# Query/key casts ahead of their differences, later steps for a pair's second head, and small VectorE/GpSimd jobs exchanged in a fused attention, conv and MLP trunk

## The chip, the cores and the metric

The kernel runs on one core of a Trainium2 chip. The metric is device time in microseconds (us) of one launch, lower is better. The engines are TensorE (PE in the profile, its weight loads PEld), VectorE (DVE), ScalarE (ACT), GpSimd (POOL) and SyncE (SP), which here issues nearly all transfers. SBUF and PSUM are the on-chip memories; only PE writes matmul results, into PSUM.

## The reference

A trunk of two residual layers on 512 rows of 1024 float32 features. Layer 0 mixes with attention, layer 1 with a short gated convolution, and each is followed by a squared-ReLU MLP. The part that the change touches is layer 0's attention: three groups with their own q, k and v for 16 heads of 64.

```python
D_MODEL = 1024; SEQ = 512; HEAD_DIM = 64
A_HEADS = 16; A_WINDOWS = (128, 512, 2048); A_DILATIONS = (1, 4, 16); A_GROUPS = 3

def mixer_a(h, w_qkv, q_gain, k_gain, w_o, cos, sin):
    qkv = (h @ w_qkv).reshape(B, S, A_GROUPS, 3, A_HEADS, HEAD_DIM)
    for g in range(A_GROUPS):
        dil = A_DILATIONS[g]
        radius = A_WINDOWS[g] // (2 * dil)
        q = partial_rope(rms_norm(qkv[:, :, g, 0], q_gain[g]), cos, sin)
        k = partial_rope(rms_norm(qkv[:, :, g, 1], k_gain[g]), cos, sin)
        v = qkv[:, :, g, 2]
        num, den, mx = dilated_group(q, k, v, dil, radius)   # banded attention
    mx = jnp.stack(mxs, 0)
    wts = jnp.exp(mx - jnp.max(mx, axis=0, keepdims=True))
    num = jnp.sum(wts[..., None] * jnp.stack(nums, 0), axis=0)
    den = jnp.sum(wts * jnp.stack(dens, 0), axis=0)
    return (num / den[..., None]).reshape(B, S, D_MODEL) @ w_o
```

partial_rope turns the first 16 dimensions of a head. The three groups share one softmax: each has its row maximum, and their numerators and denominators are weighted and added.

## The kernel before

Every large product is made in three matmuls: a float32 operand is kept as two fp32r tiles, a rounded high part and a low part (the difference), and high x high, high x low and low x high are added up in PSUM. Weights come from HBM through SP (`wraw`), ACT casts them to the high part `wh` (L292), GpSimd subtracts to make the low part `wl` (L293, called with the engine as an argument), and PE uses both. There are four `wraw` buffers and six of `wh` and `wl`.

The attention runs over 8 pairs of heads. A pair has three units of 8 k-tiles x 4 row groups r x 3 matmuls of 384 columns (L128): unit A makes q0, k0 and q1 (the digit is the group), unit B makes k1, q2 and k2, unit V makes the three v. Between these matmuls stand the small steps of the same and of the previous pair:
- `evacA`, `evacB`, `evacV` copy a unit's results from PSUM (`g`, 4 buffers) to SBUF: `rawA`, `rawB`, and the two halves of `v`. evacV calls `split`: a cast on ACT (L295), then a difference on DVE (L296).
- `norm_sq`, `norm_rs` and `norm_mul` do the RMS norm and the rotary turn, 4 row groups r each (L363 to L382). A number in the table says how many of the 4 have their turn on GpSimd (pA, pB).
- `qk_fill` transposes one of the six on PE (L391) and splits it into high and low part (ACT L295, DVE L296). k1 and k2 go into the diagonal quarters of a tile whose other quarters are zero (`zeros`), so they are split in two halves of 64 partitions each, and k0 in two pieces of 448 and 64 columns.
- `S0`, `S12` are scores (L444, L458), `exps` their exponentials (L467), `spread` and `swap` (L425, L434) bring group 0's statistics into the other groups' row order with small matmuls against a constant, `weigh1` to `weigh3` make the common softmax weights, and `weights_back` swaps group 0's part back.
- `pnorm` scales the 16 blocks of probabilities of a pair by those weights: on GpSimd (L503) or DVE (L505), 12 and 4 in the kernel before.
- `PT` transposes a scaled block (L517) and splits it into `pth` and `ptl`, `PV` multiplies it with v into `o` (L545; one buffer), for head 0 in four steps, then for head 1 in four. After a head's last PV, ACT copies half of `o` out (`tmpO`, L548), and DVE adds the two halves into `oT` (L549). The next head's first PV needs `o` free.

Everything is written out in one order before the run. Each step has a position (a number on an axis along which A, B and V each take 6, so that 1 is 16 of a unit's 96 matmuls), and a heap emits the steps between the matmuls by position. An engine takes its instructions in that order, so a step emitted early blocks what is behind it on its engine until its inputs are there:

```python
    def at(pos, fn):
        count[0] += 1
        heapq.heappush(tasks, (pos, count[0], fn))
```

The positions are sums of tA or tB (the end of a pair's unit A or B) and offsets in the table `PLACES`: row 0 for the first pair, row 1 for the second to the seventh (the middle pairs), row 2 for the last. TB places the k1, q2 and k2 fills, N0 and N12 the scalings, P, dP, gP and lP the PT and PV steps (start, spacing, extra for the second head, distance from PT to PV), X and lX the first swap, W, lW and lF the weights and the swap back, and tb the six rotary tables (`tables`, L254 and L255 on DVE).

Of the kernel before, what the change touches and what calls it, by code (L numbers as in the profile page):

```python
# [14 lines left out]
AF = mybir.ActivationFunctionType  # L15
ALU = mybir.AluOpType
# [19 lines left out]
def _constants():  # L36
# [10 lines left out]
    for n, b in enumerate((0, 1, 3)):  # L47
# [10 lines left out]


PLACES = [  # L60
    dict(sqA=0.52, rsA=0.95, mulA=2.62, dmA=0.05, TA=6.3, dT=0.2, sqB=0.08, rsB=1.22, mulB=1.8, dmB=0.1, TB=5.0, S0=1.05,
         dS=0.5, E0=2.1, X=4.2, lX=0.6, S12=7.2, dS12=0.3, E12=7.9, dE12=0.2, W=9.5, lW=0.35, lF=0.9, N0=10.85, N12=9.95,
         dN=0.04, P=11.4, dP=0.62, gP=0.4, lP=1.7, qA=0, qB=0, pA=3, pB=3, pN=1, vA=0, vB=8, xq=3.57, dxq=0.29, xs=6.25,
         lg=2.48, dlg=0.43, tb=4.26, dtb=0.21, gc=8.63),
    dict(sqA=0.02, rsA=0.87, mulA=1.79, dmA=0.28, TA=4.8, dT=0.19, sqB=0.17, rsB=0.8, mulB=1.07, dmB=0.12, TB=3.9,
         S0=0.45, dS=0.55, E0=1.1, X=3.1, lX=0.5, S12=6.5, dS12=0.24, E12=7.1, dE12=0.2, W=8.9, lW=0.35, lF=0.9, N0=10.25,
         N12=9.4, dN=0.04, P=10.9, dP=0.66, gP=0.4, lP=1.7, qA=0, qB=0, pA=0, pB=3, pN=1, vA=0, vB=12),
    dict(sqA=0.02, rsA=0.8, mulA=1.1, dmA=0.5, TA=4.5, dT=0.1, sqB=0.19, rsB=0.89, mulB=1.15, dmB=0.2, TB=3.9, S0=0.45,
         dS=0.55, E0=1.1, X=3.1, lX=0.5, S12=6.0, dS12=0.24, E12=6.5, dE12=0.18, W=8.0, lW=0.3, lF=0.7, N0=9.1, N12=8.4,
         dN=0.03, P=9.5, dP=0.36, gP=0.2, lP=0.7, qA=0, qB=0, pA=3, pB=2, pN=1, vA=0, vB=9),  # L70
]


# [1 line left out]
def trunk_kernel(ctx, tc, x, norm1, norm2, wqkv, qgain, kgain, wo, win, conv, wout, w1, w2, c_rope, c_m0, c_m12, out):  # L75
    nc = tc.nc
    pe, act, dve, pool, sync = nc.tensor, nc.scalar, nc.vector, nc.gpsimd, nc.sync
    ctx.enter_context(tc.manual_schedule())

    def ptile(p, shape, dt, name, **kw):  # L80
        return p.tile(shape, dt, name=name, **kw)

    def f32(ap):
        return ap.bitcast(F32)
# [57 lines left out]
    ones = ptile(const, [128, 128], R32, "ones")  # L142
# [38 lines left out]
    xs = dram.tile([KT, 128, S], F32, name="xs")  # L181
# [85 lines left out]

    def zeros(nm, i):
        v = f32(qk[nm][i]).rearrange("p (r h c) -> p r h c", r=4, h=2)
        dve.memset(v[0:64, :, 1], 0.0)  # L270
        dve.memset(v[64:128, :, 0], 0.0)

    box = {}

# [14 lines left out]
    def split(hi, lo, src, scale=None, eng=None):  # L289

        if scale is None:
            act.copy(hi, src)  # L292
            (eng or dve).tensor_sub(lo, src, f32(hi))  # L293
        else:
            act.activation(hi, src, AF.Copy, scale=scale)  # L295
            dve.scalar_tensor_tensor(lo, src, scale, f32(hi), op0=ALU.mult, op1=ALU.subtract)  # L296
# [87 lines left out]
    def qk_fill(raw, w, nm, ty):  # L384
        ps = ptile(psT, [128, 512], F32, "st")
        for r in range(4):
            o = ps[:, 128 * r:128 * r + 128]
            if nm[1] == "0":
                n = 32 if nm[0] == "q" else 16
                o = ps.rearrange("p (b r c) -> p r b c", r=4, c=n)[:, r]  # L390
            pe.transpose(o, raw[r][:, w, :], ident)  # L391
        hi, lo = qk[nm]
        g = cols[:, QG + ty // 2 + 3 * (ty % 2):QG + ty // 2 + 3 * (ty % 2) + 1]
        if nm[0] == "q":
            split(hi, lo, ps, g)
        elif nm == "k0":
            for d0, s0, n in ((0, 64, 448), (448, 0, 64)):
                split(hi[:, d0:d0 + n], lo[:, d0:d0 + n], ps[:, s0:s0 + n], g)
        else:
            for h in range(2):  # L400
                pp = slice(64 * h, 64 * h + 64)
                pv = ps[pp].rearrange("p (r c) -> p r c", r=4)
                hv, lv = (t[pp].rearrange("p (r h c) -> p r h c", r=4, h=2)[:, :, h] for t in (hi, lo))
                split(hv, lv, pv, g[pp])

    def q0v(t, h, b):
        return t[64 * h:64 * h + 64, 128 * b:128 * b + 128]
# [6 lines left out]
    def mx(i, n=1):  # L414

        return mxs[:, i // 8, i % 8:i % 8 + n].rearrange("p a b -> p (a b)")

    N0, D0, N0S, N12, D0S, D12, F0S, F12, NM, EX, F0 = 0, 1, 2, 3, 4, 5, 6, 7, 8, 9, 12  # L420

# [14 lines left out]

    def S0(bp):
        ps = [ptile(psT, [128, 512], F32, "st") for _ in range(2)]
        (qh, ql), (kh, kl) = qk["q0"], qk["k0"]
        for b2 in range(2):  # L440
            b = 2 * bp + b2
            for q, (a, k) in enumerate(((qh, kh), (qh, kl), (ql, kh))):
                for h in range(2):
                    pe.matmul(ps[h][:, 256 * b2:256 * b2 + 256], q0v(a, h, b), k0v(k, h, b), start=(q == 0), stop=(q == 2))  # L444
        for h in range(2):
            for b2 in range(2):
                b = 2 * bp + b2
                dve.tensor_tensor_reduce(out=sm0[:, h, b], in0=ps[h][:, 256 * b2:256 * b2 + 256],
                                         in1=msk0[:, (0, 1, 1, 2)[b]], scale=1.0, scalar=3.0e38, op0=ALU.add, op1=ALU.min,
                                         accum_out=mx(N0)[:, 4 * h + b:4 * h + b + 1])  # L450

    def S12(r):
# [6 lines left out]
        for h in range(2):  # L459
            c = slice(4 * h + r, 4 * h + r + 1)  # L460
            dve.tensor_tensor_reduce(out=sm12[:, h, r], in0=ps[:, 256 * h:256 * h + 256], in1=msk12, scale=1.0,  # L461
                                     scalar=3.0e38, op0=ALU.add, op1=ALU.min, accum_out=mx(N12)[:, c])

    def exps(g, h, b):
        t, m, d = ((sm0, N0, D0), (sm12, N12, D12))[g]
        c = slice(4 * h + b, 4 * h + b + 1)
        act.activation(t[:, h, b], t[:, h, b], AF.Exp, bias=mx(m)[:, c], scale=-1.0, accum_out=mx(d)[:, c])  # L467

    def pair_of(i):
        return mx(i, 2).rearrange("p (g n) -> p g n", g=2)  # L470
# [117 lines left out]
    def attn_tasks(p, tA, tB, c):  # L588
# [25 lines left out]
        for i, nm in enumerate(("k1", "q2", "k2")):  # L614
            put(tB + c["TB"] + c["dT"] * i, "TB", lambda i=i, nm=nm: qk_fill(rawB, i, nm, 3 + i), ("mulB", p, 4),
                ("S12", p - 1, 4))
        for i in range(2):
            put(tS + c["S0"] + c["dS"] * i, "S0", lambda i=i: S0(i), ("TA", p, 3), ("PT", p - 1, 8), ("gains", 0, 11))
            for n in range(4):
                put(tS + c["E0"] + c["dS"] * i + 0.15 * n, "E0", lambda i=i, n=n: exps(0, n // 2, 2 * i + n % 2), ("S0", p, i + 1))  # L620

# [25 lines left out]
    c = PLACES[0]  # L647
# [8 lines left out]
    for kt in range(KT):  # L656
        at(9.0 + 0.4 * kt, lambda kt=kt: sync.dma_start(xs[kt], oT[kt]))
    for i in range(4):
        at(9.0 + 0.7 * i, lambda i=i: zeros(("k1", "k2")[i // 2], i % 2))
    at(7.0, lambda: dve.memset(f32(ones), 1.0))  # L660
    at(8.8, perm_consts)
    for i in range(8):
        at(c["xq"] + c["dxq"] * i, lambda i=i: x_squares(i % 4, i // 4))
    at(c["xs"], x_stats)
# [334 lines left out]
```

## Time and profile before

| what | value |
|---|---|
| median of three runs | 1533.86 us (1533.09 to 1535.66) |
| time of the profiled execution | 1538.26 us |
| its span in the trace | 1536.4 us |
| TensorE busy | 1488.8 us, 97% of the span |
| VectorE, ScalarE, GpSimd busy | 693.0, 664.4, 727.6 us |
| data moved | 144.76 MB, 94 GB/s over the span |

The span goes from the first instruction of the profiled execution to its last. The page gives for each engine its busy time, for PE the granted clock by slices (1.00 is full), and for each wait the tile that ended it and the engine that made that tile. The stages in the trace: up to about 60 us the first unit and its preparations, then the attention pairs up to about 620 us, then the output projection, MLP, convolution and MLP.

### The profile page before, as it was taken

Reading aid. Unit: us, or ns where it says so; the run is one execution under the profiler, and the core shown is the slowest. Engines: PE = TensorE matmul, PEld = TensorE weight load, DVE = VectorE, ACT = ScalarE, POOL = GpSimd, SP = SyncE. Lnnn points to the kernel's source line nnn. Section 1 sums busy time; section 2 is a strip of 40 time slices with the busy share of each in tenths; the row PEclk is TensorE's granted clock in tenths of the full one; section 3 lists DMA queues with packets and bytes.
Section 4 is the critical chain, followed back from the end, with each engine's and each line's share of the span. In section 5 each row is a group of like instructions: output and inputs, shape, how many; then the busy total and the mean of one; then the engine's idle time right before and its main releaser. Section 6 shows DMA issues by size and latency. Waiting matters only on the chain.

```text
span 1536.4 us, 22581 instructions
## 1 busy us (share of the span) xinstructions
PE 1488.8 (97%) x7900; PEld 1296.0 (84%) x7900; DVE 693.0 (45%) x1522; ACT 664.4 (43%) x1364; POOL 727.6 (47%) x760
## 2 busy tenths in 40 slices
PE   8889999999999998999999999999999999999998
PEld 8788989999999997788888888888887888888887
DVE  5747666666657566452112032473347420121222
ACT  6445554645555555444443242433333443433320
POOL 3543544445463654354444444455454544444542
PEclk9999999999999999999999999999999999999999
DMA  6431323222232322433333333233332333333332
GB/s 149 128 95 53 110 62 100 77 86 83 80 90 63 110 62 94 129 101 99 97 93 100 97 96 96 83 90 100 100 110 82 96 97 96 96 97 96 97 96 82
DMA packets 163293, 144.76 MB, mean 94 GB/s; under 512 B 13748, under 2 KB 123116, under 8 KB 163180
## 3 DMA queue, kind: packets, MB, share of 16 engines
q1 hardware_dynamic: 162892, 143.06, 31.1%
q8 instruction: 62, 1.02, 0.3%
q14 instruction: 51, 0.42, 0.1%
q10 hardware_dynamic: 288, 0.27, 0.1%
HBM read 134.89 MB, written 8.39 MB: 93 GB/s over the span
## 4 chain that ended last, share of the span: by engine, by line
PE 59%; DVE 2%; issue 0%; DMA 0%; ACT 0%; POOL 0%; DVEq 0%
PE g L128 58%; DVE sqa L701 1%; DVE hgBl L703 0%; PE o L545 0%; PE st L517 0%; DVE hT L922 0%; PE g L855 0%; DMA out<-zr 0%; DVE zr L921 0%; PE g L715 0%; POOL sm L503 0%; DVE zr L814 0%; ACT sgh L292 0%; PE g L714 0%; DVE hgl L293 0%
## 5 line engine op out<-in xcount | busy, mean ns | idle before, releaser
L293 POOL TENSOR_TENSOR wl<-wraw,wh 128x512 fp32r<-128x512 f32 (+1 forms) x542 | 637.5, 1196 | 721.4 <-ACT wh L292 714.6
L292 ACT CAST wh<-wraw 128x512 fp32r<-128x512 f32 (+1 forms) x542 | 300.0, 570 | 542.3 <-PE g L128 412.4
L128 PE MATMUL g<-hgBl,wh 128*128 128x512 f32 x704 | 274.9, 390 | 0.0
L128 PE MATMUL g<-hgBh,wl 128*128 128x512 f32 x704 | 274.8, 390 | 0.0
L128 PE MATMUL g<-hgBh,wh 128*128 128x512 f32 x704 | 274.6, 390 | 0.0
L128 PE MATMUL g<-wh,hgh 128*128 128x384 f32 x768 | 265.2, 345 | 6.4 <-DVE v L296 6.4
L128 PE MATMUL g<-wl,hgh 128*128 128x384 f32 x768 | 264.0, 344 | 3.6 <-POOL wl L293 3.6
L128 PE MATMUL g<-wh,hgl 128*128 128x384 f32 x768 | 265.7, 346 | 1.9 <-DVE hgl L307 1.9
L791 DVE SCALAR_TENSOR_TENSOR zr<-g,R 128x512 f32<-128x512 f32 x64 | 44.2, 691 | 293.6 <-PE g L128 293.5
L128 PEld LDWEIGHTS g<-hgBh,wl 128*128 128x128 f32 x704 | 132.7, 188 | 27.9
L128 PEld LDWEIGHTS g<-hgBl,wh 128*128 128x128 f32 x704 | 132.7, 189 | 27.6
L128 PEld LDWEIGHTS g<-hgBh,wh 128*128 128x128 f32 x704 | 132.7, 188 | 27.6
L128 PEld LDWEIGHTS g<-wh,hgh 128*128 128x128 f32 x768 | 145.7, 190 | 9.0 <-DVE v L296 8.7
L128 PEld LDWEIGHTS g<-wl,hgh 128*128 128x128 f32 x768 | 145.9, 190 | 4.8 <-POOL wl L293 4.3
L128 PEld LDWEIGHTS g<-wh,hgl 128*128 128x128 f32 x768 | 145.5, 189 | 5.2 <-DVE hgl L307 3.1
L808 DVE TENSOR_TENSOR acc<-g,acc 128x512 f32<-128x512 f32 x32 | 22.1, 692 | 138.2 <-PE g L128 138.2
L128 PE MATMUL g<-z0h,wh 128*128 128x512 f32 x192 | 74.7, 389 | 0.0
L128 PE MATMUL g<-z0l,wh 128*128 128x512 f32 x192 | 74.7, 389 | 0.0
L128 PE MATMUL g<-z0h,wl 128*128 128x512 f32 x192 | 74.7, 389 | 0.0
L467 ACT ACTIVATE sm<-sm,mxs 128x256 f32<-128x256 f32 x128 | 63.7, 499 | 15.0 <-DVE mxs L461 10.2
L293 DVE TENSOR_TENSOR ptl<-st,pth 128x512 fp32r<-128x512 f32 x64 | 43.9, 688 | 50.9 <-ACT pth L292 50.1
L292 ACT CAST pth<-st 128x512 fp32r<-128x512 f32 x64 | 37.6, 588 | 64.9 <-PE st L517 64.6
(222 smaller groups left out, 2379.3 us busy)
## 6 DMA issues: line engine op xcount, KB each, us to landing
wraw<-in_mlp_w SPq DMA_DIRECT2D x256, 256.0 KB
wraw<-in_a_wqkv SPq DMA_DIRECT2D x128, 128.0 KB
wraw<-in_a_wqkv SPq DMA_DIRECT2D x64, 192.0 KB
wraw<-in_a_wqkv SPq DMA_DIRECT2D x128, 64.0 KB
wraw<-in_b_win SPq DMA_DIRECT2D x64, 128.0 KB
v0d<-v SPq DMA_DIRECT2D x8, 512.0 KB
v<-v0d SPq DMA_DIRECT2D x64, 64.0 KB
wraw<-in_a_wo SPq DMA_DIRECT2D x16, 256.0 KB
```

Source lines behind the costliest of these rows:

```text
L128: pe.matmul(unit["ps"][n][:, :width], a, b, start=st, stop=sp)
L292: act.copy(hi, src)
L293: (eng or dve).tensor_sub(lo, src, f32(hi))
L467: act.activation(t[:, h, b], t[:, h, b], AF.Exp, bias=mx(m)[:, c], scale=-1.0, accum_out=mx(d)[:, c])
L701: dve.tensor_add(state["sqa"], state["sq0"] if n == 1 else state["sqa"], sq)
L791: dve.scalar_tensor_tensor(zr, ps, 0.0, state["R"], op0=ALU.max, op1=ALU.mult)
L808: dve.tensor_add(a, ps, a)
```

## The change

- `qk_fill` first issues the casts of all its pieces on ACT and then all the differences on DVE. Before, a piece's difference stood between its cast and the next piece's cast, in the program's order.
- pN goes from 1 to 2 in all three rows: 8 of a pair's 16 scalings are on GpSimd and 8 on DVE.
- Row 1 (middle pairs): TB 3.9 to 4.05, and the steps of the second head come later (gP 0.4 to 0.9, with dP 0.66 to 0.64 and lP 1.7 to 1.6).
- Row 0 (first pair): unit A's rotary is all on DVE (pA 3 to 0), the tables start at 5.8 and not at 4.26, the k1/k2 fill is at 6.2 and not at 5.0, and S0, E0, S12, E12, W, N12, N0 and P come 0.2 to 0.6 later.
- Row 2 (last pair): unit B's rotary has three of four on GpSimd, the two swaps stand further from their spreads (lX 0.5 to 1.0, lF 0.7 to 1.0), N0 and P are 0.3 later, dP, gP and lP a little shorter.
- The zero fills of k1 and k2 (8 of 64x512 elements) and of `ones` move from DVE to GpSimd, and from positions 9.0 to 11.1 (`ones` 7.0) to 1.0 to 3.25 (`ones` 2.0). `perm_consts` moves from 8.8 to 2.0.

The code parts, and of the table one row:

```diff
@@ PLACES, row 1 @@
-    dict(sqA=0.02, rsA=0.87, mulA=1.79, dmA=0.28, TA=4.8, dT=0.19, sqB=0.17, rsB=0.8, mulB=1.07, dmB=0.12, TB=3.9,
+    dict(sqA=0.02, rsA=0.87, mulA=1.79, dmA=0.28, TA=4.8, dT=0.19, sqB=0.17, rsB=0.8, mulB=1.07, dmB=0.12, TB=4.05, S0=0.45,
...
-         N12=9.4, dN=0.04, P=10.9, dP=0.66, gP=0.4, lP=1.7, qA=0, qB=0, pA=0, pB=3, pN=1, vA=0, vB=12),
+         dN=0.04, P=10.9, dP=0.64, gP=0.9, lP=1.6, qA=0, qB=0, pA=0, pB=3, pN=2, vA=0, vB=12),
...
@@ zeros @@
-        dve.memset(v[0:64, :, 1], 0.0)
-        dve.memset(v[64:128, :, 0], 0.0)
+        pool.memset(v[0:64, :, 1], 0.0)
+        pool.memset(v[64:128, :, 0], 0.0)
@@ qk_fill @@
         if nm[0] == "q":
-            split(hi, lo, ps, g)
+            parts = [(hi, lo, ps, g)]
         elif nm == "k0":
-            for d0, s0, n in ((0, 64, 448), (448, 0, 64)):
-                split(hi[:, d0:d0 + n], lo[:, d0:d0 + n], ps[:, s0:s0 + n], g)
+            parts = [(hi[:, d0:d0 + n], lo[:, d0:d0 + n], ps[:, s0:s0 + n], g) for d0, s0, n in ((0, 64, 448), (448, 0, 64))]
         else:
+            parts = []
             for h in range(2):
                 pp = slice(64 * h, 64 * h + 64)
                 pv = ps[pp].rearrange("p (r c) -> p r c", r=4)
-                hv, lv = (t[pp].rearrange("p (r h c) -> p r h c", r=4, h=2)[:, :, h] for t in (hi, lo))
-                split(hv, lv, pv, g[pp])
+                parts.append(tuple(t[pp].rearrange("p (r h c) -> p r h c", r=4, h=2)[:, :, h] for t in (hi, lo)) + (pv, g[pp]))
+        for h_, l_, v, sc in parts:
+            act.activation(h_, v, AF.Copy, scale=sc)
+        for h_, l_, v, sc in parts:
+            dve.scalar_tensor_tensor(l_, v, sc, f32(h_), op0=ALU.mult, op1=ALU.subtract)
@@ the steps of the first pair @@
-        at(9.0 + 0.7 * i, lambda i=i: zeros(("k1", "k2")[i // 2], i % 2))
-    at(7.0, lambda: dve.memset(f32(ones), 1.0))
-    at(8.8, perm_consts)
+        at(1.0 + 0.75 * i, lambda i=i: zeros(("k1", "k2")[i // 2], i % 2))
+    at(2.0, lambda: pool.memset(f32(ones), 1.0))
+    at(2.0, perm_consts)
```

**Where instructions move.** First ACT's queue in the second pair, at the fills of k1, q2 and k2, with each instruction's waits; before:

```order
L295 ACTIVATE k1h<-st,cols 64x4x128 [waits PE_49]
L295 ACTIVATE k1h<-st,cols 64x4x128 [waits DVE_49]
L295 ACTIVATE q2h<-st,cols 128x512 [waits PE_49]
L295 ACTIVATE k2h<-st,cols 64x4x128 [waits PE_49]
L295 ACTIVATE k2h<-st,cols 64x4x128 [waits DVE_49]
L292 CAST wh<-wraw 128x384 [waits DMAHW4_49,DMAHW3_49,Pool_49]
```

and of the change, the same place:

```order
L405 ACTIVATE k1h<-st,cols 64x4x128 [waits PE_49]
L405 ACTIVATE k1h<-st,cols 64x4x128
L405 ACTIVATE q2h<-st,cols 128x512 [waits PE_49]
L405 ACTIVATE k2h<-st,cols 64x4x128 [waits PE_49]
L405 ACTIVATE k2h<-st,cols 64x4x128
L292 CAST wh<-wraw 128x384 [waits DMAHW4_49,DMAHW3_49,Pool_49]
```

The order is the same, and the second half of k1 and of k2 no longer waits for DVE.

Second, GpSimd's queue at the start of the program, after the identity matrix; `wl` are the weights' low parts and the tiles with a P are the rotary's temporaries of the first pair's unit A. Before:

```order
L293 TENSOR_TENSOR wl<-wraw,wh 128x384 x14
L379 TENSOR_TENSOR tmpR1P<-rawA_108,tabA 128x96
L380 TENSOR_TENSOR tmpR2P<-rawA_108,tabA 128x6x8
L381 TENSOR_TENSOR tmpR2P<-rawA_108,tabA 128x6x8
L382 TENSOR_TENSOR rawA_108<-tmpR1P,tmpR2P 128x6x16
```

and of the change:

```order
L293 TENSOR_TENSOR wl<-wraw,wh 128x384
L270 MEMSET k1h 64x4x128
L271 MEMSET k1h 64x4x128
L293 TENSOR_TENSOR wl<-wraw,wh 128x384
L270 MEMSET k1l 64x4x128
L271 MEMSET k1l 64x4x128
L663 MEMSET ones 128x128
L293 TENSOR_TENSOR wl<-wraw,wh 128x384
L270 MEMSET k2h 64x4x128
L271 MEMSET k2h 64x4x128
...
L293 TENSOR_TENSOR wl<-wraw,wh 128x384 x17
```

Twelve rotary instructions that stood between two runs of `wl` (three row groups of four) are gone from this queue, and nine fills stand between the first `wl`.

Third, DVE's queue in the second pair around the add that frees `o` after the first head; `rawA_109` to `rawA_111` are row groups 1 to 3 of the next pair's unit A, L373 their norm, L379 to L382 their rotary. Before:

```order
L373 TENSOR_TENSOR rawA_110<-rawA_110,stA 128x384
L379 TENSOR_TENSOR tmpR_2423<-rawA_110,tabA 128x96
L380 TENSOR_TENSOR tmpR_2424<-rawA_110,tabA 128x6x8
L381 TENSOR_TENSOR tmpR_2424<-rawA_110,tabA 128x6x8
L382 TENSOR_TENSOR rawA_110<-tmpR_2423,tmpR_2424 128x6x16
L549 TENSOR_TENSOR oT_75<-o,tmpO 64x512
L293 TENSOR_TENSOR ptl<-st,pth 128x512
```

and of the change:

```order
L373 TENSOR_TENSOR rawA_110<-rawA_110,stA 128x384
L379 TENSOR_TENSOR tmpR_2414<-rawA_110,tabA 128x96
L380 TENSOR_TENSOR tmpR_2415<-rawA_110,tabA 128x6x8
L381 TENSOR_TENSOR tmpR_2415<-rawA_110,tabA 128x6x8
L382 TENSOR_TENSOR rawA_110<-tmpR_2414,tmpR_2415 128x6x16
L293 TENSOR_TENSOR ptl<-st,pth 128x512
L552 TENSOR_TENSOR oT_75<-o,tmpO 64x512
L373 TENSOR_TENSOR rawA_111<-rawA_111,stA 128x384
```

The add still stands behind row group 2's rotary, and one `ptl` difference has moved ahead of it. On PE, five matmuls of a unit more stand ahead of the second head's first PV than before.

## Rows read from the trace of the kernel before

**Rows 1.** Windows: length, busy (instructions) of PE, PEld, DVE, ACT, POOL, clock, DMA share, GB/s.

```profile
48.00:60.00 12.00, 6.72 (x32) 5.57 (x30) 8.96 (x21) 3.42 (x8) 8.53 (x14) 0.86 0.50 163
60.00:130.00 70.00, 63.78 (x414) 60.87 (x415) 42.16 (x125) 34.85 (x87) 32.03 (x46) 0.95 0.31 92
130.00:554.00 424.00, 409.93 (x2842) 390.12 (x2841) 276.18 (x776) 234.70 (x566) 209.66 (x300) 1.00 0.29 83
554.00:627.00 73.00, 63.99 (x405) 55.22 (x404) 43.91 (x110) 38.50 (x88) 29.82 (x37) 0.95 0.32 101
627.00:1168.00 541.00, 540.78 (x2382) 446.59 (x2381) 195.79 (x269) 201.75 (x351) 266.29 (x214) 1.00 0.32 97
```

**Rows 2.** Waits of PE: for which tile of which engine; us in total, times, longest.

```profile
PE g L128 <- DVE v L296: 7.6, 8, 1.6
PE o L545 <- DVE oT L549: 6.9, 6, 1.6
PE st L517 <- POOL sm L503: 5.4, 8, 2.9
PE st L434 <- DVE spread L425: 4.4, 3, 2.1
PE g L128 <- POOL wl L293: 3.6, 2, 3.5
...
PE st L391 <- POOL rawB L382: 2.3, 6, 0.4
...
PE g L128 <- DVE hgl L307: 1.9, 2, 1.7
PE st L444 <- ACT k0h L295: 1.6, 1, 1.6
```

**Rows 3.** Timeline, fourth pair: start, duration, instruction [idle before, what ended it].

```profile
292.44 0.69 ACT L295 ACTIVATE k1h<-st,cols 64x512 fp32r<-64x512 f32 x1 [0.81 <-DVE k1l L296]
298.33 0.44 PE L128 MATMUL g<-wh,hgh 128*128 128x384 f32 x1 [0.81 <-DVE v L296]
```

**Rows 4.** Timeline, the scalings and PE's waits for them: first and fourth pair.

```profile
101.61 0.93 PE L517 MATMUL st<-ident,sm 128*128 128x128 f32 x3 [2.94 <-POOL sm L503]
...
312.51 5.14 POOL L503 TENSOR_SCALAR sm<-sm,mxs 128x256 f32<-128x256 f32 x11 [0.57 <-DVE mxs L492]
312.55 1.06 DVE L505 TENSOR_SCALAR sm<-sm,mxs 128x256 f32<-128x256 f32 x2
315.88 0.78 PE L517 MATMUL st<-ident,sm 128*128 128x128 f32 x3 [0.22 <-POOL sm L503]
```

**Rows 5.** Timeline, fourth pair, around the second head's first PV: PE, DVE, GpSimd.

```profile
329.96 0.26 DVE L379 TENSOR_TENSOR tmpR<-rawA,tabA 128x96 f32<-128x96 f32 x1
332.89 2.08 POOL L293 TENSOR_TENSOR wl<-wraw,wh 128x384 fp32r<-128x384 f32 x2 [5.12 <-ACT wh L292]
333.14 0.95 DVE L379 TENSOR_TENSOR tmpR<-rawA,tabA 128x96 f32<-128x96 f32 x1
334.52 0.34 PE L128 MATMUL g<-wh,hgh 128*128 128x384 f32 x1
334.70 0.34 PE L128 MATMUL g<-wl,hgh 128*128 128x384 f32 x1
336.10 0.39 PE L545 MATMUL o<-pth,v 128*128 128x256 f32 x1 [1.06 <-DVE oT L549]
```

**Rows 6.** Timeline, first pair: tables, last low part, first norm, q0's transposes.

```profile
26.32 1.01 DVE L254 TENSOR_TENSOR tabA<-rope,gb 128x32 f32<-128x32 f32 x1
26.61 0.59 ACT L306 COPY oT<-st 128x512 f32<-128x512 f32 x1
28.39 0.73 DVE L307 SCALAR_TENSOR_TENSOR hgl<-oT,cols,hgh 128x512 fp32r<-128x512 f32 x1
45.42 0.56 DVE L373 TENSOR_TENSOR rawA<-rawA,stA 128x384 f32<-128x384 f32 x1
53.19 1.05 PE L391 MATMUL st<-ident,rawA 128*128 128x128 f32 x4
```

More of the change, by code (lines that the diff above doesn't have):

```diff
@@ L60 @@
 PLACES = [
[L61 to L64, printed above, removed]
-    dict(sqA=0.02, rsA=0.87, mulA=1.79, dmA=0.28, TA=4.8, dT=0.19, sqB=0.17, rsB=0.8, mulB=1.07, dmB=0.12, TB=3.9,
-         S0=0.45, dS=0.55, E0=1.1, X=3.1, lX=0.5, S12=6.5, dS12=0.24, E12=7.1, dE12=0.2, W=8.9, lW=0.35, lF=0.9, N0=10.25,
-         N12=9.4, dN=0.04, P=10.9, dP=0.66, gP=0.4, lP=1.7, qA=0, qB=0, pA=0, pB=3, pN=1, vA=0, vB=12),
-    dict(sqA=0.02, rsA=0.8, mulA=1.1, dmA=0.5, TA=4.5, dT=0.1, sqB=0.19, rsB=0.89, mulB=1.15, dmB=0.2, TB=3.9, S0=0.45,
-         dS=0.55, E0=1.1, X=3.1, lX=0.5, S12=6.0, dS12=0.24, E12=6.5, dE12=0.18, W=8.0, lW=0.3, lF=0.7, N0=9.1, N12=8.4,
-         dN=0.03, P=9.5, dP=0.36, gP=0.2, lP=0.7, qA=0, qB=0, pA=3, pB=2, pN=1, vA=0, vB=9),
+    dict(sqA=0.52, rsA=0.95, mulA=2.62, dmA=0.05, TA=6.3, dT=0.2, sqB=0.08, rsB=1.22, mulB=2.1, dmB=0.1, TB=6.2, S0=1.25,
+         dS=0.65, E0=2.4, X=4.2, lX=0.6, S12=7.8, dS12=0.3, E12=8.4, dE12=0.2, W=10.0, lW=0.35, lF=0.9, N0=11.35, N12=10.45,
+         dN=0.04, P=11.9, dP=0.6, gP=0.5, lP=1.6, qA=0, qB=0, pA=0, pB=3, pN=2, vA=0, vB=8, xq=3.57, dxq=0.29, xs=6.25,
+         lg=2.48, dlg=0.43, tb=5.8, dtb=0.3, gc=8.63),
+    dict(sqA=0.02, rsA=0.87, mulA=1.79, dmA=0.28, TA=4.8, dT=0.19, sqB=0.17, rsB=0.8, mulB=1.07, dmB=0.12, TB=4.05, S0=0.45,
+         dS=0.55, E0=1.1, X=3.1, lX=0.5, S12=6.5, dS12=0.24, E12=7.1, dE12=0.2, W=8.9, lW=0.35, lF=0.9, N0=10.25, N12=9.4,
+         dN=0.04, P=10.9, dP=0.64, gP=0.9, lP=1.6, qA=0, qB=0, pA=0, pB=3, pN=2, vA=0, vB=12),
+    dict(sqA=0.02, rsA=0.8, mulA=1.1, dmA=0.5, TA=4.5, dT=0.1, sqB=0.17, rsB=0.8, mulB=1.07, dmB=0.12, TB=4.05, S0=0.45,
+         dS=0.55, E0=1.1, X=3.1, lX=1.0, S12=6.0, dS12=0.24, E12=6.5, dE12=0.18, W=8.0, lW=0.3, lF=1.0, N0=9.4, N12=8.4,
+         dN=0.03, P=9.8, dP=0.34, gP=0.15, lP=0.6, qA=0, qB=0, pA=3, pB=3, pN=2, vA=0, vB=9),
 ]
```

## The prediction, made before the changed kernel was run

> **What bounds the kernel now.** I read the windows by stage first. From 627 us on PE is busy 540.78 of 541 us [rows 1], and the change moves nothing there, so only the attention can gain: length less PE's busy time leaves, of the earlier windows, 424.00 - 409.93 = 14.1 us of PE idle in the six middle pairs, 70.00 - 63.78 = 6.2 around the first pair's scores, 12.00 - 6.72 = 5.3 just before, and 73.00 - 63.99 = 9.0 in the last pair and its tail [rows 1]. The clock column adds to that. A mean of 0.95 over 70 us means about 7 us at 1.2 instead of 2.4 GHz, which costs some 3.5 us; 0.86 over 12 us means 3.4 us at that level, a cost of 1.7; the middle pairs run at 1.00 [rows 1]. Next the list of PE's waits says what each gap waits for [rows 2], and then the timeline of one middle pair what the releaser itself had waited for [rows 3 to 5]. The kernel is bound by PE, with some four short stops in each pair and a cluster of long ones in the first and the last; a term counts only where it takes one of these stops away or makes one.
>
> A stop costs a little more than its idle time: the first matmul behind it takes 0.44 where others take 0.34 [rows 3, 5]. I add 0.1.
>
> **Middle pairs.** *V.* PE stops 0.81 for the low part of v [rows 3], and over all pairs 7.6 in 8 stops, the longest 1.6 [rows 2]. The first pair has that longest one, six middle pairs make 4.9, and 1.1 is left for the last. Before it, ACT stood 0.81 between the halves of k1, for DVE's difference [rows 3], and the same wait stands between the halves of k2; the v casts are behind both in ACT's queue. Without them the casts of v can start up to 1.6 earlier, and DVE's differences, which no longer alternate with ACT, at least 0.8. That covers the 0.81. Gain 0.9 for each of six pairs; if DVE gains less than I think, the bound is nothing.
>
> *Scalings.* GpSimd takes 5.14 / 11 = 0.47 for one, DVE 1.06 / 2 = 0.53 beside it [rows 4]. PE waits 0.22 [rows 4]. GpSimd's eight now end at 312.51 + 3.7 = 316.2, and the block that the first transposes need from it, its fifth, at 314.9. DVE's order is four of group 1 and 2, the copy behind the swap (some 0.2), and two of group 0: 312.55 + 2.1 + 0.2 + 1.0 = 315.8, where PE was ready at 315.88 - 0.22 = 315.7. So DVE becomes the one that is waited for, by about 0.1. Gain 0.2 to 0.3; bounds 0 and 0.5.
>
> *Second head.* PE stops 1.06 for the add that frees `o` [rows 5]; five of these in the middle pairs make 5.3 of the 6.9, and the first pair has the 1.6 [rows 2]. The second head's first PV comes five matmuls later, each started 0.18 after the one before [rows 5]: 0.9. But the add stands behind row group 2's rotary in DVE's queue, and one low part of the probabilities has moved from a place ahead of row group 1 to one right ahead of the add. That part needs a PE transpose which is itself later. DVE there is slow because of GpSimd: the same rotary instruction takes 0.26 alone and 0.95 while two `wl` of 1.04 run [rows 5]. From nothing (the add slides along) to 1.2 (the stop goes) I take 0.5, nearer to nothing than to all, since the add has not moved ahead of anything.
>
> *Against it.* The pair's last PV is now about 0.9 closer to the next pair's first scores. ACT's copy of `o` and DVE's add behind it stand in the two queues ahead of unit B's squares and sums, so the rotary of B ends later, and PE already waits up to 0.4 for it in six pairs [rows 2]. The k1 fill is two matmuls (0.35) later, which takes up part. Cost 0.25, from 0 to 0.9.
>
> Net 0.9 + 0.3 + 0.5 - 0.25 = 1.45 in five pairs and 0.95 in the sixth (it has no second-head stop): **8.2 us**, bounds 3 and 15.
>
> **First pair.** *Up to q0's transposes (at 53.19 before [rows 6]).* The last low part of x started at 28.39, though its input was there at 26.61 + 0.59 = 27.20 [rows 6]; with the tables behind it, PE's stop of 1.7 [rows 2] is 1.1 shorter. The stop of 3.5 for `wl` [rows 2] goes as well, since twelve rotary instructions leave GpSimd's queue. By PE alone q0's transposes would start near 53.2 - 1.1 - 3.6 - 0.3 = 48. They can't: DVE now does everything. The tables start about 2 us later, and they and the rotary run into more `wl`. A table multiplication beside a `wl` takes 1.01 [rows 6], with neighbours of about 0.2; four more such meetings are 3.3 us. The first norm, at 45.42 before [rows 6], then starts near 50.8. Four row groups follow, each a norm of 0.56 [rows 6] and a rotary whose widest instruction is 0.26 [rows 5], together some 1.3, and 0.5 for the end: 56.5. So q0's transposes come 3.3 later than before, and the gains ahead of them are lost in that. If there are no more meetings than before it is nothing; if each rotary meets one as well it is 6.
>
> *Behind them.* The stop of 1.6 for k0's second piece [rows 2] goes with the cast order: 1.8 back, since two stops' refills go. The clock is low after such a stop already; a longer one may cost 0 to 1.7 more, I take 0.4. Together +3.3 - 1.8 + 0.4 = **1.9 us lost**.
>
> *Fills.* Nine fills go to GpSimd ahead of `wl`. They delay `wl` where PE has them six deep, and the low parts of x on DVE might be held by them as table multiplications are by a `wl`, at 0.8 each [rows 6]; I take nothing, since two `wl` are already used up before. The Trainium skill, "SBUF — State Buffer", section "Who interferes with whom", says that a DVE instruction with two SBUF inputs contends with a GpSimd instruction that reads SBUF and not with one that only writes; no row here has a fill on GpSimd beside DVE, and by the rule the term is nothing too.
>
> *Later stops.* V 1.6 + 0.1 [rows 2] goes, as the k1 fill now comes behind v: 1.7. The scalings' stop of 2.94 [rows 4] is that of six GpSimd scalings behind two `wl`; half of it is DVE's now and no `wl` stands between: 3.1 with its neighbours. With it goes the low clock of this window, 3.5 us by the rows above; if a stop of some length stays, so does that. The second head's 1.6 becomes about 0.5: 1.1. Net for the pair 1.7 + 3.1 + 3.5 + 1.1 - 1.9 = **7.5 us**, bounds 1 and 12.
>
> **Last pair.** V: 1.2. The two swaps' stops are 2.1 each (4.4 in three [rows 2]). The first swap now comes behind k1's transposes, 0.5 of a position later (8 matmuls of 0.18, 1.4 us), but those wait for B's rotary themselves: 0.7. The swap back, 0.3 later, gains 0.9. The scalings' stop, 5.4 - 2.94 - 6 x 0.22 = 1.1 [rows 2, 4], goes down to 0.1: 1.0. Its tail behind the last PV has no cover and doesn't change. **3.8 us**, bounds 1 and 6.
>
> **Sum.** 8.2 + 7.5 + 3.8 = 19.5. The profiled execution took 1538.26 (span 1536.4), so it would take 1518.8; the median of the three runs lies 4.4 below it at 1533.86, which gives 1514. What a measurement can tell from no change is 0.2%, 3.1 us.
>
> **The rivals.**
> - *More comes* (chance 0.22). The second-head stop goes fully (0.7 more in five pairs, 3.5), and q0's transposes are no later than before (3.3): 1507. For it: 0.9 of delay against an idle time of 1.06. Against it: the add has the same work ahead of it.
> - *Less comes* (0.15). No gain at the second head (2.5), q0's transposes 3 later still with 1.3 more at 1.2 GHz, a stop of 0.25 at the scalings that stays (2): 1523. For it: every stop that is taken from PE in a pair lets it arrive earlier at the next one.
> - *The scalings shut each other out* (0.07). If a DVE scaling can't run while GpSimd's run, DVE's four more in a pair end about 1 us later than I have, and PE waits for them: 8 us, 1522. Against it: DVE did two in 1.06 while GpSimd kept to 0.47 each [rows 4]. The Trainium skill, same page and section, has the rule: copies and tensor_scalar can run on DVE in a mode with the port pair it shares with GpSimd, and the one that issues second blocks fully until the other's instruction ends. The trace shows at most some sharing, as said.
> - *Slower* (0.06). One mechanism: the end of the second head, moved towards the next pair's scores, pushes unit B's squares, rotary and k1 fill back in every pair. I priced this at 0.25. To cancel the rest it must cost (19.5 + 7 x 0.25) / 7, about 3 us a pair; at 4 us the time is 1514 + 7 x 3.75 = 1540. Only the queue order of ACT speaks for it; the stop at that place is 0.4 [rows 2], and PE stops there for nothing else.
>
> My forecast has 0.50. The range from 1504 to 1525 holds it and the first three rivals, and leaves out the slower one and the far ends of the bounds. Faster: all but the slower case and a rest of 0.04 that falls within 0.2%.
>
> **What would show it.** In the trace of the changed kernel: no stop of PE for v; k1's and k2's casts back to back; the stop at the second head's first PV near 0.6; stops for `rawB` of about 0.6; a stop of several us for `rawA` before q0's transposes and a low clock behind it; no long stop for scalings in the first pair and a clock near 1.00 in its window; the last pair's swaps near 1.2. The prediction is wrong if the first pair's scalings still stop PE long enough to bring the clock down, if a stop appears at a scaling on DVE in every pair, or if `rawB` costs PE over 1 us a pair.

## The result and the profile after

The changed kernel takes 1515.35 us (median, 1514.98 to 1515.53); before it is 1534.76 in the same comparison. The ratio is 0.9872, with a 95% interval from 0.9855 to 0.9889: 1.3% faster. The forecast was 1514. The span of the profiled execution goes from 1536.4 to 1513.6 us. In the table of experiments one execution of e8, which took 3794.75 us where the others took about 1510, is left out.

The windows of the changed kernel, columns as in [rows 1] (the last pair ends some 22 us sooner, so the last window ends at 605 and not at 627):

```profile
48.00:60.00 12.00, 5.58 (x20) 4.54 (x20) 9.98 (x35) 2.96 (x7) 1.25 (x2) 0.60 0.60 196
60.00:130.00 70.00, 69.17 (x485) 66.08 (x484) 50.07 (x141) 40.32 (x96) 32.80 (x44) 1.00 0.28 82
130.00:554.00 424.00, 418.57 (x2913) 400.65 (x2911) 294.75 (x837) 239.73 (x586) 205.67 (x289) 1.00 0.29 84
554.00:605.00 51.00, 44.71 (x277) 37.45 (x278) 30.66 (x63) 27.32 (x58) 22.16 (x23) 0.97 0.39 127
```

In the middle window PE idles 5.4 of 424 us where it idled 14.1, and in the first pair's window 0.8 of 70 where it idled 6.2, with the granted clock at 1.00 and not 0.95. The window before that got worse: 6.4 us idle of 12 where it was 5.3, and a clock of 0.60 where it was 0.86. PE's waits, to be read against [rows 2]:

```profile
PE st L391 <- DVE cols L263: 3.5, 1, 3.5
...
PE st L437 <- DVE spread L428: 3.0, 7, 1.4
PE st L391 <- DVE rawA L382: 2.9, 3, 1.3
...
PE st L391 <- DVE k1l L407: 1.6, 1, 1.6
PE g L128 <- DVE v L296: 1.6, 2, 1.0
PE o L548 <- DVE oT L552: 1.5, 5, 0.6
...
PE st L391 <- POOL rawB L382: 0.8, 1, 0.8
PE st L520 <- DVE sm L508: 0.6, 1, 0.6
```

Stops for v fell from 7.6 us in 8 to 1.6 in 2, for oT from 6.9 to 1.5, for scalings from 5.4 to under 1; new are 3.5 and 2.9 before and between q0's transposes and 1.6 for k1 in the last pair. The stops for `rawB` in the six middle pairs (2.3 in all) are gone; the 0.8 that is left is the last pair's. The start of the first, second and last pair's scores cuts the run into stages. Timeline of PE, changed kernel:

```profile
61.95 0.38 PE L447 MATMUL st<-k0h,q0h 64*128 64x256 f32 x2
...
128.51 0.39 PE L447 MATMUL st<-k0h,q0h 64*128 64x256 f32 x2
...
540.20 0.39 PE L447 MATMUL st<-k0h,q0h 64*128 64x256 f32 x2
```

and before:

```profile
59.91 0.76 PE L444 MATMUL st<-k0h,q0h 64*128 64x256 f32 x2 [1.63 <-ACT k0h L295]
...
135.87 0.39 PE L444 MATMUL st<-k0h,q0h 64*128 64x256 f32 x2
...
559.39 0.39 PE L444 MATMUL st<-k0h,q0h 64*128 64x256 f32 x2
```

So up to the first scores 2.0 us are lost; from there to the second pair's 9.4 are gained (75.96 to 66.56), over the next six periods 11.8 (423.52 to 411.69), and from the last pair's scores to the end of the span 3.6 (977.0 to 973.4). The forecast had 1.9 lost (for the stretch up to and just behind them), 9.4 gained, 8.2 gained, 3.8 gained.

The last 3.6 has two parts. The last PV matmul starts at 617.45 before and at 595.87 in the changed kernel, 58.06 and 55.67 behind the last pair's scores, a gain of 2.4. The other 1.2 lies behind it, where the two programs are the same. The ten us behind the last PV, before and after:

```profile
617.45:627.45 10.00, 7.71 (x23) 5.64 (x22) 4.13 (x6) 3.96 (x7) 1.26 (x1) 0.66 0.66 225
```

```profile
595.87:605.87 10.00, 7.40 (x27) 5.57 (x26) 4.17 (x6) 4.02 (x7) 1.27 (x1) 0.83 0.67 230
```

PE stops there for the same 2.04 us in both, and the granted clock is 0.66 and 0.83. In e4, e5, e8, e10 and e12 it is 1.00 behind the same stop, and from the last PV to the end takes 915.5 to 915.6 us where it takes 917.7 in the changed kernel and 919.0 before. What decides this no run shows; up to 3.4 us of a difference between two traces can come from it.

### The profile page after: what moved, and what is told of

It is laid out like the page before. It is cut to its first block, busy times and chain, and to the rows that moved or that the text cites. A ratio compares the mean times of both kernels' runs of the same rounds, so it can differ in the third digit from the quotient of the medians.

```text
span 1513.6 us, 22622 instructions
## 1 busy us (share of the span) xinstructions
PE 1483.0 (98%) x7900; PEld 1293.4 (85%) x7900; DVE 706.4 (47%) x1553; ACT 664.8 (44%) x1364; POOL 716.4 (47%) x729
## 4 chain that ended last, share of the span: by engine, by line
PE 77%; DVE 11%; issue 5%; POOL 3%; ACT 2%; DMA 1%; SPq 1%; POOLq 0%; ACTq 0%; DVEq 0%
PE g L128 72%; PE st L461 1%; PE o L548 1%; PE st L520 1%; PE st L391 1%; POOL wl L293 1%; DMA wraw<-in_a_wqkv 1%; DVE sm L451 1%; DVE rawA L373 1%; DVE ptl L293 1%; DVE stA L156 1%; DVE stA L155 1%; DVE sqa L704 1%; SPq L571 1%; ACT wh L292 0%
```

## The experiments

All ratios are against the kernel before; the changed kernel's own is 0.9872 (0.9855 to 0.9889). Kernels were run in several groups, so the ratio is what compares them, and where the intervals overlap, the trace says how far a part can be told. There is one trace of each kernel. The changed kernel and e2, e3, e6, e7 and e8 run the same steps up to the first scores, and these start between 61.17 and 62.55; a smaller difference at that place tells nothing.

| run | median us | ratio, 95% interval |
|---|---|---|
| e1 casts undone | 1523.97 | 0.9927 (0.9914 to 0.9941) |
| e2 scalings undone | 1521.42 | 0.9918 (0.9904 to 0.9931) |
| e3 second head undone | 1518.58 | 0.9894 (0.9881 to 0.9908) |
| e4 first pair's row undone | 1516.88 | 0.9885 (0.9872 to 0.9899) |
| e5 tables together | 1514.03 | 0.9863 (0.9851 to 0.9876) |
| e6 last pair's row undone | 1516.30 | 0.9874 (0.9862 to 0.9887) |
| e7 rotary B, 2 of 4 on GpSimd | 1530.72 | 0.9967 (0.9955 to 0.9978) |
| e8 add ahead of the rotary | 1508.51 | 0.9832 (0.9820 to 0.9845) |
| e9 unit B's tables late | 1514.51 | 0.9864 (0.9849 to 0.9878) |
| e10 e8 and e9 | 1507.88 | 0.9819 (0.9804 to 0.9833) |
| e11 fills undone | 1516.83 | 0.9876 (0.9860 to 0.9893) |
| e12 casts alone | 1526.69 | 0.9927 (0.9914 to 0.9941) |

The theory is the forecast's own: every part takes away the stop that it was costed against, for the reason given. The rival is that parts do each other's work, above all that later positions or an earlier PE decide, and not the part named.

**Casts (e1, e12).** e1 undoes them in the changed kernel, e12 makes them alone in the kernel before.

```diff
         for h_, l_, v, sc in parts:
             act.activation(h_, v, AF.Copy, scale=sc)
-        for h_, l_, v, sc in parts:
             dve.scalar_tensor_tensor(l_, v, sc, f32(h_), op0=ALU.mult, op1=ALU.subtract)
```

e1: 

> The changed kernel, with the cast and the difference of each piece again one after the other. Theory (casts first is what takes the stop for v away): PE's stops for v, 1.6 us in 2 in the changed kernel, go back to about 7 us in 7 or 8, and the stop for the second piece of k0 comes back with 1.6: 8 us slower than the changed kernel's 1515.35, 1523. Rival (the k1 fill moved behind v in the first pair and two matmuls later in the middle ones does it): no more than 3 us slower, 1518, with stops for v of 0.2 to 0.4 at most.

e12 (the lines of qk_fill as in the change, and nothing else): 

> The kernel before with the order of casts and differences in qk_fill as the only change. Theory (it takes the stops for v away by itself, as its undoing brought them back): the stops for v go from 7.6 in 8 to under 2, that for k0's second piece goes; 8 to 9 us faster than before, 1525.5. Rival (it gives this only together with the later k1 fill and the other scalings): stops for v of 3 or more stay, or the time comes back as longer stops at the second head or the scalings; 3 to 5 us faster, 1530.

In e1 the stop for v is back, in PE's list of waits:

```profile
PE g L128 <- DVE v L296: 7.1, 6, 1.3
```

and so is its cause, in ACT's timeline of a middle pair's fills:

```profile
354.05 0.68 ACT L405 ACTIVATE k1h<-st,cols 64x512 fp32r<-64x512 f32 x1 [0.81 <-DVE k1l L406]
356.99 0.68 ACT L405 ACTIVATE k2h<-st,cols 64x512 fp32r<-64x512 f32 x1 [0.97 <-DVE k2l L406]
```

The ratio rises by 0.0055, 8.6 us in the medians, as the theory said; the rival is out. The stop for k0 did not come back in e1; v's is the bulk of it, and spread, oT and k2 add 0.7, 0.9 and 0.8 of stops. Alone (e12) the part is worth 0.0073, 11.2 us of its group's 1537.91 (in the other groups the kernel before has 1534.5 to 1535.0). Its waits:

```profile
PE o L548 <- DVE oT L552: 7.8, 6, 2.1
PE st L437 <- DVE spread L428: 4.2, 2, 2.1
PE st L520 <- POOL sm L506: 3.6, 8, 1.3
...
PE g L128 <- DVE v L296: 1.7, 3, 0.8
```

The stops for v fell from 7.6 to 1.7, the one for oT grew by 0.9, and the longest stop for scalings, in the first pair, fell from 2.9 to 1.3 though the scalings are shared as before. By stages e12 gains 1.0 up to the first scores, 2.3 from there to the second pair's, 4.7 in the middle pairs, loses 0.5 from the last pair's scores to its last PV, and gains 3.4 behind that, where its program is that of the kernel before and the clock is 1.00 and not 0.66. So some 7.5 us go with the casts, near what was expected; the rest of the 11.2 is not shown to be theirs.

**Scalings (e2).** `pN=2` back to `pN=1` in the three rows of the table.

> The changed kernel with 12 of 16 scalings on GpSimd again (pN=1 in all rows). Theory (the shares are what takes the stops for scalings away): 0.57 comes back in six pairs, 1 in the last, 3.1 in the first and with it the low clock behind that stop, 3.5: 11 us slower, 1526. Rival (the first pair's long stop came from its order and positions, which stay changed): the first pair stops under 0.7 us and its clock stays at 1.00 behind it, 4.5 us slower, 1520.

Measured 6.1 us slower than the changed kernel, between the two. Each middle pair stops 0.26 for a scaling again, the last 1.2 (the changed kernel's stops 0.6 there, for one on DVE), and the first 1.03 (0.24), the row of PE's timeline in e2:

```profile
100.24 0.79 PE L520 MATMUL st<-ident,sm 128*128 128x128 f32 x3 [1.03 <-POOL sm L506]
```

Its clock stays at 1.00 from 60 to 130 us. So the shares are worth some 0.5 a middle pair (the fourth takes 68.82 from scores to scores and not 68.29), where the forecast had 0.3, and most of the long stop of the first pair, with the low clock behind it, is not theirs. Where it came from can be read in the kernel before: GpSimd's six scalings stood behind two low parts of weights, these behind two casts, and those behind a transfer. GpSimd and ACT, before:

```profile
98.56 1.06 ACT L292 CAST wh<-wraw 128x384 fp32r<-128x384 f32 x2 [5.55 <-DMA wraw<-in_a_wqkv]
99.15 1.95 POOL L293 TENSOR_TENSOR wl<-wraw,wh 128x384 fp32r<-128x384 f32 x2 [2.11 <-ACT wh L292]
101.07 2.74 POOL L503 TENSOR_SCALAR sm<-sm,mxs 128x256 f32<-128x256 f32 x6
```

and in e12, where only the casts differ:

```profile
95.72 1.08 ACT L292 CAST wh<-wraw 128x384 fp32r<-128x384 f32 x2 [3.92 <-DMA wraw<-in_a_wqkv]
96.31 1.97 POOL L293 TENSOR_TENSOR wl<-wraw,wh 128x384 fp32r<-128x384 f32 x2 [0.49 <-ACT wh L292]
98.26 2.75 POOL L506 TENSOR_SCALAR sm<-sm,mxs 128x256 f32<-128x256 f32 x6
```

The scalings themselves take as long in both; GpSimd's wait for a weight went from 2.1 to 0.5. ACT stood 5.55 and 3.92 for the transfer. PE's stop is shorter by 1.6, and so is GpSimd's wait. Why the transfer came sooner was not tried. In e1, with the casts undone and the rest of the change in place, the stop does not come back either, so that the casts are not the only part that can take it away.

**Second head (e3, e8).** e3 puts its steps back alone. e8 does that and instead moves unit A's rotary, so that the add into oT comes ahead of row groups 1 to 3 in DVE's queue.

```diff
-... N12=9.4, dN=0.04, P=10.9, dP=0.64, gP=0.9, lP=1.6, ...
+... N12=9.4, dN=0.04, P=10.9, dP=0.66, gP=0.4, lP=1.7, ...
 (e8 as well:)
-    dict(sqA=0.02, rsA=0.87, mulA=1.79, dmA=0.28, TA=4.8, ...
+    dict(sqA=0.02, rsA=0.87, mulA=2.4, dmA=0.28, TA=4.8, ...
```

e3: 

> The changed kernel with the second head's steps of the six middle pairs at their old places (gP, dP, lP of row 1 alone). Theory (the later place hides the add into oT): the stop for oT goes from 0.15 to 0.6 back to about 1.06 in five pairs, 4.5 us slower, 1520; if something is given back at rawB, 0.3 a pair less. Rival (DVE reaches the add sooner because of the other parts): at most 1 us slower, 1516.

e8: 

> The changed kernel with the second head's steps of the middle pairs at their old places, and unit A's rotary 0.61 of a position later (mulA 1.79 to 2.4), so that the add into oT stands ahead of row groups 1 to 3 in DVE's queue and not behind row group 2. Theory (the stop for oT is the rotary ahead of the add; the later second head pays at the next pair's spread and rawB): oT's stop goes below 0.3 without the later steps, and the stops of 0.29 and 0.04 at spread and rawB go too: 1512. Rival (the add is late for another reason): the stop is 1.06 again, 1518.

The second head's first PV in e3 and in the changed kernel, each a row of PE's timeline in the second pair:

```profile
186.41 0.39 PE L548 MATMUL o<-pth,v 128*128 128x256 f32 x1 [1.06 <-DVE oT L552]
```

```profile
186.08 0.39 PE L548 MATMUL o<-pth,v 128*128 128x256 f32 x1 [0.16 <-DVE oT L552]
```

So the later place gains 0.9 at the stop. The median of e3 is 3.2 us above that of the changed kernel; the intervals just overlap, but a stop of 1.06 stands in four pairs of the trace and one of 1.74 in a fifth (0.60 in the changed kernel). The 3.2 is less than five times 0.9, because the later place has a price: the changed kernel stops 0.29 for `spread` in its middle pairs, where e3 does not, and in e3 the stops for `spread` are two in the whole run. e8 takes away both. Its list of PE's waits has no row for oT and none for a middle pair's spread but one:

```profile
PE g L128 <- DVE v L296: 1.7, 2, 1.3
PE st L391 <- DVE k1l L407: 1.6, 1, 1.6
...
PE st L437 <- DVE spread L428: 1.6, 2, 1.4
```

and DVE's timeline shows the add ahead of the rotary, with row group 0 in front of it and not three row groups:

```profile
315.07 0.26 DVE L379 TENSOR_TENSOR tmpR<-rawA,tabA 128x96 f32<-128x96 f32 x1
316.21 0.68 DVE L552 TENSOR_TENSOR oT<-o,tmpO 64x512 f32<-64x512 f32 x1 [0.36 <-ACT tmpO L551]
317.43 1.28 DVE L373 TENSOR_TENSOR rawA<-rawA,stA 128x384 f32<-128x384 f32 x1
```

Now the add waits for ACT's copy alone. 1508.51 is 6.8 us below the changed kernel, with intervals that don't meet. In the traces 4.0 of it lie in the middle pairs (407.73 for 411.69), and 2.1 behind the last PV, where the clock is 1.00 and not 0.83 and the programs are the same. The stop was the rotary in DVE's queue, and the change hid it by delay where moving the rotary removes it.

**First pair (e4, e5, e9, e11).** e4: row 0 of the table as before (8 scalings on DVE), fills, ones and perm_consts as before. e11: the eight fills alone. e5: dtb 0.3 to 0.02, all tables at once. e9: unit B's three tables later:

```diff
-        at(c["tb"] + c["dtb"] * i, lambda i=i: tables(i))
+        at(c["tb"] + c["dtb"] * i if i < 3 else 12.35 + 0.2 * (i - 3), lambda i=i: tables(i))
```

e4: 

> The changed kernel with the first pair's row of the table as before (but 8 scalings on DVE) and with the fills of k1, k2 and ones and perm_consts on DVE and at their old places. Theory (the first pair's new row costs at q0's transposes and gains nothing that casts and scalings don't give alone): the first scores start near 58, some 4 us sooner than the changed kernel's 61.95; with up to 2 us given back at v, 2 to 4 us faster, 1512. Rival (the later places of the first pair's row are what takes its stops away): the first pair stops again for v and for scalings by 1 to 3 us with a low clock behind, 4 us slower or more, 1519 to 1522.

e5: 

> The changed kernel with all 48 table multiplications right behind the last low part of x (dtb 0.3 to 0.02), ahead of the row statistics, where GpSimd makes only one low part. Theory (DVE's queue decides when the first scores start, and its tables meet low parts of weights on GpSimd): the first norm starts near 46.5 and not at 49.97, the first scores 2 to 3.5 us sooner than 61.95, 1512. Rival (the squares on ACT or the transfers decide): no change, 1515.

e9: 

> The changed kernel with the three tables of unit B (24 of the 48 multiplications) between the differences of q0, k0 and q1, where DVE waits anyway and GpSimd has nothing, instead of in unit A's chain; the two small inputs of the tables lie in buffers that the probabilities use later. Theory (DVE's queue sets the start of the first scores, and long runs of tables hold up GpSimd's low parts): the chain loses 2.5 us of tables and some four meetings with low parts, no stop of 3 for a low part as with the tables together; first scores 2 to 4 us sooner than 61.95, 1512. Rival (something else than DVE's queue is as late): first scores at 61 or later, 1515.

e11: 

> The changed kernel with the eight fills of k1 and k2 on DVE again, at their old positions, which are behind row group 3's rotary. Theory (forecast: on GpSimd they cost nothing; on DVE 5 us of them stand ahead of the copy of unit B's results and of q0's difference): the first scores 2 to 4 us later than 61.95, 1518. Rival (other waits there cover them, as DVE has gaps of 1.08 and 0.36): 1515.5.

In e4 the first scores start at 58.99, 3.0 sooner than in the changed kernel, as the theory said. But then the stops come that the later places had removed; PE in e4:

```profile
80.68 0.44 PE L128 MATMUL g<-wh,hgh 128*128 128x384 f32 x1 [0.82 <-DVE v L296]
...
99.16 0.33 PE L520 MATMUL st<-ident,sm 128*128 128x128 f32 x1 [1.48 <-POOL sm L506]
...
119.46 0.39 PE L548 MATMUL o<-pth,v 128*128 128x256 f32 x1 [2.09 <-DVE oT L552]
```

and the second pair's scores are at 130.88, 2.4 later than in the changed kernel. The early scores are worth 3.0 and the stops behind them 5.3 (2.2 of that may be the fills', if they cost here what they cost in e11 below); both sides were half right. By the medians the two kernels can't be told apart.

e5 moved DVE's chain as expected (first norm 46.51 and not 49.97), but the first scores only from 61.95 to 60.49: a new stop of 3.0 for a low part of weights stood ahead of them, with a clock of 0.91 from 30 to 48 us where it was 1.00. GpSimd in e5, where one low part otherwise takes 1.0:

```profile
28.44 4.84 POOL L293 TENSOR_TENSOR wl<-wraw,wh 128x384 fp32r<-128x384 f32 x1 [1.69 <-ACT wh L292]
```

e9 has no such stop, first norm at 46.49, first scores at 60.43, 1.5 sooner and not 2 to 4; the 24 tables now take DVE's time between q0's and q1's differences. e11 puts the first scores at 62.63, which is not told apart from the 62.55 of e6, and the second pair's 2.9 later, 2.2 of that behind the first scores: fills on DVE have a price, and what is shown of it is paid there. None of e5, e9 and e11 differs from the changed kernel by its interval; only the traces tell them apart.

**Last pair (e6).** Row 2 as before, with pN=2.

> The changed kernel with the last pair's row of the table as before, but 8 scalings on DVE. Theory (the forecast's: later swaps hide part of their spreads): the two swaps' stops go back from 0.2 and 1.4 to about 2.1 each, k1's new stop of 1.6 goes: 1 to 2 us slower, 1517. Rival (what the swaps win is lost at k1's transposes): no change, 1515.

PE's waits for spread are 5.9 in 8 (3.0 in 7 in the changed kernel), those for k1 and for `rawB` are gone. From the last pair's first scores to its last PV it takes 56.57 us against 55.67, so that the row is worth 0.9: most of what the swaps win is lost at the transposes of unit B, as the rival has it, and some is left, as the theory has it. (To the end of the span the two are 973.6 and 973.4, but behind the last PV the programs are the same.) By the medians the two can't be told apart.

**The two stops for v that are left (e7).** pB=3 to pB=2 in row 1.

> The changed kernel with two instead of three of four row groups of unit B's rotary on GpSimd in the middle pairs. The stops for v that are left, in the second and the sixth pair, stand behind a weight cast that waits for its transfer, and the transfers wait for buffers that GpSimd's low parts free behind the rotary. Theory (that chain): with four instructions less ahead of the low parts the two stops of 0.6 and 1.0 go; the DVE rotary may cost 0.3 a pair at rawB: 1514 to 1517. Rival (the two stops are DVE's own): they stay or grow.

The chain as the changed kernel's timeline has it in the sixth pair, ACT's cast, ACT's v, PE:

```profile
421.88 0.52 ACT L292 CAST wh<-wraw 128x384 fp32r<-128x384 f32 x1 [1.49 <-DMA wraw<-in_a_wqkv]
422.42 2.00 ACT L295 ACTIVATE v<-g,small 128x384 fp32r<-128x384 f32 x4
...
423.71 0.44 PE L128 MATMUL g<-wh,hgh 128*128 128x384 f32 x1 [0.98 <-DVE v L296]
```

The row of waits names DVE's v, but ACT waited for a transfer one step earlier. In e7 both stops are gone, but this proves little: each middle pair now stops 1.9 to 2.0 for `spread`, since DVE does a second row group's rotary ahead of it, and a PE that comes later may by itself give the transfer the time. PE's waits in e7:

```profile
PE st L437 <- DVE spread L428: 11.9, 6, 2.0
```

It took 15 us more than the changed kernel, far outside what either theory said. Ten of them are these stops; in the middle window the clock is also 0.98 and not 1.00. Why the transfer is late stays open.

**Both improvements (e10).**

> The late tables of unit B together with the add ahead of row groups 1 to 3 (second head at its old places, mulA 2.4). Theory (the two are separate places of the program): their gains add up, 1509.5 less 2 to 4, 1506.5. Rival (an earlier first pair meets later stops): 1509.

1507.88 us, ratio 0.9819 (0.9804 to 0.9833): faster than both kernels of the study. Against e8 the intervals overlap; by the medians 0.6 us more came from the late tables, by the spans of the traces 0.9 (1505.7 and 1506.6). That is less than the theory had, and too little to be shown.

## Why the prediction was right

The forecast lay 1.4 us from the time. That it came so close is in part luck: two errors cancel. From one profiled execution to the other the sum had 19.5, down to 1518.8; the execution took 1515.53, and the spans differ by 22.8. The sum was 3.3 short, nearly all of it in the middle pairs (11.8 for 8.2). Then 4.4 were taken off because the profiled execution of the kernel before lay that far above its median, but that of the changed kernel lies only 0.2 above its own (1515.53 and 1515.35). The sum had already booked 3.5 for a low clock in that one execution, so part of the 4.4 may have been counted twice; no trace of a faster execution of the kernel before was kept that could show it. By stages, several terms are right, and some for other reasons.

- *V, middle pairs*: forecast 0.9 in six pairs, for ACT's wait between the halves. Shown by e1 and e12. Two pairs keep a stop, of 0.57 and 0.98, where ACT waits for a weight; they take 1.6 off the 5.4.
- *Scalings, middle pairs*: forecast 0.3 a pair. e2 brings back a stop of 0.26, and some 0.5 a pair from scores to scores. That DVE would be waited for by 0.1 did not show: no middle pair stops for one.
- *Second head*: forecast 0.5 between nothing and 1.2, priced low "since the add has not moved ahead of anything". It gained 0.9 at the stop itself. The term was mis-sized: from e3 to the changed kernel the add ended only 0.3 later against the pair's scores (the second head's first PV starts 57.25 and 57.57 behind them in the second pair), while PE came 1.2 later. This, the scalings and `rawB` below are what the middle pairs gained beyond 8.2.
- *Against it*: forecast 0.25 at rawB, with stops of about 0.6 there. This step failed in its place: a price of the right size stands at `spread` (0.29) and is removed in e3 and e8, but at `rawB` the list of waits has no stop of a middle pair where each had 0.38, a gain of 2.3 that the sum does not have. It stays gone with the casts, the shares, the second head, the first or the last pair's row undone (e1 to e4, e6), and e12 still has it; what is left of the change is TB, the k1 fill two matmuls (0.35) later. No run undoes that alone, so this is by exclusion.
- *First pair up to the scores*: forecast 1.9 lost, with the first norm near 50.8 and transposes behind several us of stop. Measured 2.0; the first norm ran at 49.97 and the stops were 3.5 and 2.9, with a clock of 0.60 in the window. The first half is as stated: table and small statistics instructions met low parts of weights, at 0.92 to 1.01 each. But again two terms cancel. q0's last transposes end at 56.28 where they ended at 54.24, 2.0 later and not 3.3. And the 1.8 that the cast order was to bring back at k0 did not come: with the casts alone (e12) PE stops there for 0.94 and 0.62, before for 1.63, with the casts and the old row (e4) 0.56, and with the casts undone and the new row (e1) there is no such stop. So the stop went with the later places, and no time came back for it.
- *First pair, scalings and clock*: 3.1 + 3.5 were booked to the shares. This step failed, though its sum is in the result: with the shares undone (e2) the clock stays up and the stop is 1.03, and with the casts alone (e12) it is 1.3 with a clock of 0.98 in that window. The stop held 2.1 us in which GpSimd waited for a weight. e4 shows that the first pair's row and the fills also carry part: without them 1.5 comes back.
- *Fills at nothing*: e11 shows that the move is worth something, 2.2 us behind the first scores in the trace, since on DVE they would stand in its queue. That they cost nothing on GpSimd agrees with it, but was not tried by itself.
- *Last pair*: 3.8 forecast, 3.6 measured, but only 2.4 of it up to the last PV. The terms were too large: 1.6 for the swaps is 0.9 for the whole row (e6), 1.0 for the scalings is 0.5 (e2, 56.17 for 55.67), and 1.2 for v is 0.8 (e1, 56.51). The other 1.2 is the clock behind the last PV, of which the forecast said that nothing changes there.
- *The scalings shut each other out*: did not happen. DVE's eight lie beside GpSimd's, and no middle pair stops for them.

## What to carry to other kernels

When PE waits for an engine, read that engine's queue and not its busy time: a small add of 0.7 us behind three row groups of rotary stopped PE for 1.06, and changing the order (e8) gave 4.0 us more in the middle pairs than giving it more time. A forecast, and a stage of it, can be right while its parts are not; undo each part, and make the largest alone, before crediting one. Read a run that does better than expected by its stages, too: in e8 and e12 2.1 and 3.4 us of the gain lie where nothing was changed. And a releaser in the list of waits is only the last step: for the first pair's scalings and the last stops for v, the timeline of the releaser showed a weight transfer behind it.

## What the runs showed that I had not expected

- *A run of short DVE instructions held up GpSimd for as long as it lasted.* In e5, 48 table multiplications, started about 0.10 us apart, ran without one being stretched, while GpSimd's low part beside them took 4.84 us and not 1.0. In the kernel before, a multiplication that met a low part already running took 1.01 [rows 6]. The Trainium skill, "SBUF — State Buffer", section "Who interferes with whom", says that the order of issue decides which of two contenders is held, not the operation; the trace of the kernel before agrees (the low part started at 26.21, the multiplication that took 1.01 at 26.32). In e5 it was the run of multiplications that started first, at 27.43, and the low part came at 28.44; but multiplications from 28.45 on were not held either, so that a run of overlapping short instructions kept the other engine out throughout.
- *The clock multiplies a cluster's price.* With the stops before q0's transposes the granted clock of that window was 0.60 instead of 0.86: (1 - 0.60) x 12 = 4.8 us of full speed withheld where it was 1.7. Part of it falls on stops and costs nothing, so 3.1 more is an upper bound; the forecast had taken 0.4. In e2, with the same stops, the clock of that window was 0.72, so that it is not fixed by them alone.
- *A rotary group moved from GpSimd to DVE stopped PE 2.0 us a pair and not 0.29* (e7), at one place, because it stood ahead of a single instruction (`spread`, 0.30 us in the changed kernel's third pair and 1.01 in e7's) that PE needs.
